# Small products of three token mixers on TensorE: other shapes and another order of the parts of the array

## The chip, the core and the metric

The kernel runs on one core of one Trainium2 chip. The metric is the device time of one execution in microseconds (us), as the median of several runs. TensorE (PE) multiplies a stationary operand, which a weight load (PEld) brings into the 128 x 128 array, with a moving operand that streams through it; results land in PSUM. VectorE (DVE), ScalarE (ACT) and GpSimd (POOL) do the elementwise work, SyncE (SP) issues the DMAs.

## What is computed

One decoder layer on 1024 tokens of width 1024, all in float32. The middle of it is three groups of heads of size 64 side by side: two chunked gated linear attentions (HGRN2 with 4 heads, GLA with 6) and RWKV-7 (6 heads).

```python
h = x * (1.0 + scale1) + shift1
z = h @ w_in[l]                                   # 1024 x 1024 by 1024 x 3984
o_h = hgrn2_mixer(z_h, ...); o_g = gla_mixer(z_g, ...); o_r = rwkv7_mixer(z_r, ...)
o = jnp.concatenate([o_h, o_g, o_r], axis=-1) @ w_out[l]
x = layer_norm(DEEPNORM_ALPHA * x + (1.0 + gate1) * o, ...)
h = x * (1.0 + scale2) + shift2
m = jnp.square(jax.nn.relu(h @ mlp_w_up[l])) @ mlp_w_down[l]     # width 4096
x = layer_norm(DEEPNORM_ALPHA * x + (1.0 + gate2) * m, ...)

# linear attention, per head and chunk
scores = jnp.einsum('bthk,bshk,btshk->bths', qc, kc, decay)      # causal
o = einsum('bths,bshv->bthv', scores, vc) + einsum('bthk,bhkv->bthv', qc * jnp.exp(b), S)
S = S * jnp.exp(b_end)[..., None] + einsum('bshk,bshv->bhkv', kc * jnp.exp(b_end[:, None] - b), vc)
# RWKV-7, per head and token
S = S * w_t + (S a_t) b_t^T + v_t k_t^T;   y_t = S r_t
```

## The kernel before

The 1024 tokens are two blocks of 512, and a block is four tiles of 128 tokens. Two kinds of work share the engines.

**Dense products** are the projections and the MLP. Each operand is split into two float32r parts, and a product is three matmuls (`mm3`, L1270 to L1272) of a 128 x 128 stationary operand and 512 moving columns, into PSUM tiles `dn` (and `tn` at the end). ACT makes the high part of a weight slab (L1220), DVE the low part (L1221).

**Mixers** run on one tile of 128 tokens at a time, in plain float32. Their matmuls are small. A float32 matmul of the program shows as two records in the trace, a transpose as one. Heads go in pairs, head a = 0 on partitions 0 to 63 and a = 1 on 64 to 127. Linear attention uses PSUM tiles `ml`, RWKV-7 `mr`, two buffers each.

- `la_blocks` (L512): scores of the second 64 tokens against the first 64. Per head one matmul of 64 rows and 64 columns, the two heads of a pair into two PSUM tiles; ACT copies them out (L515). The right factor `R` holds both heads of a pair, with zeros where a head meets the other head's rows.
- `la_attn`: the outputs of ten heads. For each pair one product of the decayed queries with the state (L475, whole array, 128 moving columns) and for each of its two heads two products of the scores `sc` with the values `V` (L482): one for the first 64 tokens on 64 rows, one for the second on 128 rows. ACT copies the sums out (L484).
- `rw_prep`: `BK` holds b~ and k~ of a chunk and a second copy of k~ (made by ACT, L585), so that both heads can take them in the order they need. The chunk products (L598) take 64 rows, 128 columns and 128 moving columns, the heads of a pair in turn.
- `rw_prep2`: `BK` transposed, head by head (L662, 64 rows), three at a time into a PSUM tile, each copied out by ACT (L664).
- `rw_chain`: after the second chunk of a tile the outputs `y`. For each head a and chunk d three products with the state (L795, a quarter of the array), then three with u and v (L798, 128 rows and half of the columns). ACT copies them out (L800).

`mixers` runs RWKV-7 a tile ahead of linear attention. `Order` sets the order of each engine's queue ahead of the run: it goes through a planned time with its own costs (`cost`), and of the instructions that are ready there it takes the one of the lowest level and the earliest traced one. The first block's mixers have level 0, and the second block's projection fills the room between them; the second block's mixers lie between chunks of the first block's MLP. Semaphores wait for data as usual.

## Time and profile before

| what | value |
|---|---|
| median of 3 runs | 1686.83 us |
| the runs | 1665.26, 1686.83, 1694.75 us |
| profiled execution, first to last instruction | 1676.5 us |
| PE busy | 1565.6 us (93%) |
| DVE, ACT, POOL busy | 65%, 41%, 25% |
| chain that ended last, by engine | PE 49%, DVE 6%, ACT 1%, POOL 1%, DMA 1% |

The profiled execution was timed by its span alone; the span lies 10.3 us below the median and inside the range of the runs. The chain that ended last could be followed back to 671.6 us. The first block's mixers lie between some 100 us and 671 us, the second block's between 671 us and 1050 us; after that there are dense products alone.

### The profile page before, as it was taken

The page shows a single profiled execution, that of the slowest core. Times are in us where ns is not written, and L with a number is a line of the kernel's source. Part 1 is how long each engine was busy: PE and PEld are TensorE (multiplying, and loading weights), DVE is VectorE, ACT ScalarE, POOL GpSimd, SP SyncE. Part 2 cuts the span into 40 slices and gives each one's busy share as a digit, 9 for nine tenths or more (in the row PEclk, how much of TensorE's full clock was granted, in tenths as well). Part 3 has the DMA queues.
Part 4 walks back from the last instruction along what each step waited for, and adds up shares of the span by engine and source line. Part 5 has one row for each costly group of instructions (what it writes and reads, how often), then busy time and mean ns, then how long its engine had stood idle before and what let it go on. Part 6 is the DMA issues. An engine that isn't in the chain of part 4 may idle for free.

```text
span 1676.5 us, 29172 instructions
## 1 busy us (share of the span) xinstructions
PE 1565.6 (93%) x11002; PEld 1220.9 (73%) x11002; DVE 1097.7 (65%) x1877; ACT 683.0 (41%) x1415; POOL 419.1 (25%) x561
## 2 busy tenths in 40 slices
PE   6998988999989998889999999999999999999996
PEld 5887766666667876657667676778888888888885
DVE  8796586666657448875857766555766954444477
ACT  3452343444344655544534543442333333333241
POOL 5224054263434132451452624100000000000003
PEclk9999996787879999898959989999999999999998
DMA  9997542313322456522313131444523643333331
GB/s 310 324 335 232 181 134 68 108 51 110 87 65 86 130 176 194 178 63 77 88 37 105 39 101 44 146 132 130 191 95 94 201 144 96 96 97 96 94 120 50
DMA packets 164892, 214.03 MB, mean 128 GB/s; under 512 B 41456, under 2 KB 91792, under 8 KB 164752
## 3 DMA queue, kind: packets, MB, share of 16 engines
q1 hardware_dynamic: 164752, 212.18, 40.5%
q8 instruction: 86, 1.41, 0.3%
q14 instruction: 54, 0.44, 0.1%
HBM read 180.07 MB, written 32.06 MB: 127 GB/s over the span
## 4 chain that ended last, share of the span: by engine, by line
PE 49%; DVE 6%; DMA 1%; issue 1%; ACT 1%; POOL 1%; SPq 0%; DVEq 0%; ACTq 0%; POOLq 0%
PE dn L1272 10%; PE dn L1271 9%; PE dn L1270 9%; PE tn L1272 4%; PE tn L1271 4%; PE tn L1270 4%; PE ml L482 1%; DVE Rs L425 1%; PE ml L475 1%; PE mr L798 1%; PE mr L795 1%; DVE xt L1401 1%; DVE wl L1221 0%; DMA lnr<-in_ln_b_dram 0%; PE ml L434 0%
## 5 line engine op out<-in xcount | busy, mean ns | idle before, releaser
L1220 ACT CAST wh<-raw 128x512 fp32r<-128x512 f32 (+2 forms) x424 | 253.2, 599 | 558.4 <-PE dn L1272 230.7
L1221 DVE TENSOR_TENSOR wl<-raw,wh 128x512 fp32r<-128x512 f32 (+2 forms) x408 | 284.8, 703 | 274.0 <-ACT wh L1220 246.0
L1270 PE MATMUL dn<-wh,ah 128*128 128x512 f32 (+1 forms) x736 | 288.0, 393 | 6.8 <-DVE xt L1417 3.8
L1271 PE MATMUL dn<-wl,ah 128*128 128x512 f32 (+1 forms) x736 | 288.0, 391 | 2.0 <-DVE wl L1221 2.0
L1272 PE MATMUL dn<-wh,al 128*128 128x512 f32 (+1 forms) x736 | 285.1, 394 | 1.8 <-DVE al L1443 1.8
L1270 PE MATMUL dn<-ah,wh 128*128 128x512 f32 x560 | 236.7, 424 | 19.6 <-ACT ah L1263 11.7
L1271 PE MATMUL dn<-al,wh 128*128 128x512 f32 x560 | 236.7, 423 | 3.2 <-DVE al L1221 1.6
L1272 PE MATMUL dn<-ah,wl 128*128 128x512 f32 x560 | 236.8, 424 | 0.0
L1270 PEld LDWEIGHTS dn<-wh,ah 128*128 128x128 f32 x736 | 140.7, 191 | 36.8 <-ACT wh L1220 3.5
L1271 PEld LDWEIGHTS dn<-wl,ah 128*128 128x128 f32 x736 | 140.3, 191 | 29.6 <-DVE wl L1221 3.4
L1272 PEld LDWEIGHTS dn<-wh,al 128*128 128x128 f32 x736 | 140.0, 191 | 29.5 <-DVE al L1443 3.2
L1270 PEld LDWEIGHTS dn<-ah,wh 128*128 128x128 f32 x560 | 111.8, 200 | 44.4 <-ACT ah L1263 11.7
L1271 PEld LDWEIGHTS dn<-al,wh 128*128 128x128 f32 x560 | 112.0, 200 | 30.3 <-DVE al L1264 4.1
L1272 PEld LDWEIGHTS dn<-ah,wl 128*128 128x128 f32 x560 | 111.8, 200 | 23.6 <-issue 0.4
L416 POOL TENSOR_TENSOR ld<-b 128x640 f32<-128x640 f32 x56 | 76.5, 1373 | 138.0 <-PE ml L512 15.3
L1458 DVE TENSOR_TENSOR xt<-xt,dn 128x512 f32<-128x512 f32 x104 | 67.1, 683 | 52.9 <-PE dn L1272 52.8
L1272 PE MATMUL tn<-ah,wl 128*128 128x512 f32 x256 | 100.8, 394 | 0.0
L1271 PE MATMUL tn<-al,wh 128*128 128x512 f32 x256 | 100.2, 391 | 0.0
L1270 PE MATMUL tn<-ah,wh 128*128 128x512 f32 x256 | 99.6, 389 | 0.0
L1518 POOL TENSOR_SCALAR lnm<-lnm 128x1 f32<-128x1 f32 x3 | 2.1, 684 | 328.5 <-DVE lnm L1516 328.5
L425 DVE TENSOR_TENSOR Rs<-ld,Q 64x320 f32<-64x320 f32 x112 | 82.0, 732 | 2.0 <-ACT ld L157 0.6
L1186 DVE SCALAR_TENSOR_TENSOR xt<-xt,xt 128x1024 f32<-128x1024 f32 x48 | 64.2, 1344 | 16.3 <-DMA xt<-in_ada_wt_dram 16.0
(290 smaller groups left out, 2500.9 us busy)
## 6 DMA issues: line engine op xcount, KB each, us to landing
raw<-in_mlp_w_up_dram SPq DMA_DIRECT2D x128, 256.0 KB
raw<-in_mlp_w_down_dram SPq DMA_DIRECT2D x128, 256.0 KB
xt<-in_ada_wt_dram SPq DMA_DIRECT2D x48, 512.0 KB
raw<-in_w_in_dram SPq DMA_DIRECT2D x64, 256.0 KB
raw<-in_w_in_dram SPq DMA_DIRECT2D x48, 192.0 KB
raw<-in_w_out_dram SPq DMA_DIRECT2D x32, 256.0 KB
raw<-in_w_in_dram SPq DMA_DIRECT2D x32, 196.0 KB
raw<-in_xt_dram SPq DMA_DIRECT2D x24, 256.0 KB
```

The lines of the kernel that those rows point to most:

```text
L416: nc.gpsimd.tensor_tensor(ev, bv, bv[:, :, h - 1:h].broadcast_to([P, 5 * nb, 2 * h]), ALU.subtract)
L425: nc.vector.tensor_tensor(Rv[half[a], a], ev[half[a], :, up], qv[half[a], :, up], ALU.mult)
L475: nc.tensor.matmul(po[:, c0:c0 + 128], qe[:, p, :], St[:, p, :], start=True, stop=False, skip_group_check=True)
L482: nc.tensor.matmul(po[half[t], c0 + 64 * a:c0 + 64 * a + 64], sc[r, 2 * p + a, half[t]], V[r, v0:v0 + 64], start=False, stop=True, skip_gr ...
L795: nc.tensor.matmul(py[half[d], p * 64:p * 64 + 64], AR[rr, p, d, 1, :], s["SU"][d][rr, p, a, :], start=(p == 0), stop=False, skip_group_ch ...
L1186: nc.vector.scalar_tensor_tensor(w, w, 1.0, self.cact, ALU.mult, ALU.mult, accum_out=self.sums[:, q:q + 1])
L1220: nc.scalar.copy(hi[:, 0:n], src)
L1221: (eng or nc.vector).tensor_tensor(lo[:, 0:n], src, hi[:, 0:n].bitcast(F32), ALU.subtract)
L1270: nc.tensor.matmul(ps, lh, rh, start=first, stop=False)
L1271: nc.tensor.matmul(ps, lh, rl, start=False, stop=False)
L1272: nc.tensor.matmul(ps, ll, rh, start=False, stop=last)
L1458: nc.vector.tensor_tensor(acc[t][:, cs], acc[t][:, cs], ps, ALU.add)
```

## The change

The same sums are computed. Six places use other shapes or another order.

```diff
 (la_attn: scores times values)
                 for a in range(2):
                     v0 = p * 128 + 64 * a
-                    for t in range(2):
-                        r = slice(0, 64 + 64 * t)
-                        nc.tensor.matmul(po[half[t], c0 + 64 * a:c0 + 64 * a + 64], sc[r, 2 * p + a, half[t]],
-                                         V[r, v0:v0 + 64], start=False, stop=True, skip_group_check=True)
+                    nc.tensor.matmul(po[:, c0 + 64 * a:c0 + 64 * a + 64], sc[:, 2 * p + a, :], V[:, v0:v0 + 64],
+                                     start=False, stop=True, skip_group_check=True)
 (la_blocks, h == 64)
-            pss = [self.lps() for _ in range(2)]
-            for p in range(5):
-                for a in range(2):
-                    r = slice(64 * a, 64 * a + 64)
-                    nc.tensor.matmul(pss[a][0:64, p * 64:p * 64 + 64], e[r, p * 128:p * 128 + 64], R[r, a, p, :],
-                                     start=True, stop=True)
-            for a in range(2):
-                nc.scalar.copy(sc[0:64, a::2, 64:128], pss[a][0:64, 0:320].rearrange("p (q t) -> p q t", q=5))
+            ps = self.lps()
+            for p, j in ((0, 0), (3, 1), (1, 0), (4, 1), (2, 0)):
+                c0 = (p - 3 * j) * 128
+                for m in range(2):
+                    s0 = 64 * j + 32 * m
+                    nc.tensor.matmul(ps[s0:s0 + 32, c0:c0 + 128], e[:, p * 128 + 32 * m:p * 128 + 32 * m + 32],
+                                     R[:, :, p, :], start=True, stop=True)
+            for j, h0, h1 in ((0, 0, 6), (1, 6, 10)):
+                nc.scalar.copy(sc[0:64, h0:h1, 64:128], ps[64 * j:64 * j + 64, 0:64 * (h1 - h0)]
+                               .rearrange("p (q t) -> p q t", t=64))
 (rw_prep)
-        BK = self.mt([P, 3, 2, 3, 64], "BK")
+        BK = self.mt([P, 3, 2, 2, 64], "BK")
...
-        nc.scalar.copy(BKm[:, :, 2, :], BKm[:, :, 0, :])
...
             for p in range(3):
-                for a in range(2):
-                    rr = slice(64 * a, 64 * a + 64)
-                    nc.tensor.matmul(pxs[a][:, p * 128:(p + 1) * 128],
-                                     BK[rr, p, c, 1 - a:3 - a, :].rearrange("p x t -> p (x t)"),
-                                     AR[rr, p, c].rearrange("p x t -> p (x t)"), start=True, stop=True)
+                for x in range(2):
+                    for a in range(2):
+                        rr = slice(64 * a, 64 * a + 64)
+                        r = slice(64, 128) if a ^ x else slice(0, 64)
+                        nc.tensor.matmul(pxs[a][r, p * 128:(p + 1) * 128], BK[rr, p, c, x, :],
+                                         AR[rr, p, c].rearrange("p x t -> p (x t)"), start=True, stop=True)
 (rw_prep2, per chunk c)
-            for a in range(2):
-                rr = slice(64 * a, 64 * a + 64)
-                pt = self.mps()
-                for p in range(3):
-                    nc.tensor.transpose(pt[:, p * 64:(p + 1) * 64],
-                                        BK[rr, p, c, 1 - a:3 - a, :].rearrange("p x t -> p (x t)"), self.ident[rr, rr])
-                nc.scalar.copy(BT[:, a], pt[:, 0:192].rearrange("p (q d) -> p q d", d=64))
+            pt = self.mps()
+            for p in range(3):
+                nc.tensor.transpose(pt[:, p * 128:(p + 1) * 128], BK[:, p, c].rearrange("p x t -> p (x t)"), self.ident)
+            pt3 = pt[:, 0:384].rearrange("p (q d) -> p q d", d=128)
+            nc.scalar.copy(BT[:, 0], pt3[:, :, 0:64])
+            for x in range(2):
+                nc.scalar.copy(BT[64 - 64 * x:128 - 64 * x, 1], pt3[64 * x:64 * x + 64, :, 64:128])
 (rw_chain, c == 1)
+            pys = [self.mps() for _ in range(2)]
+            for p in range(3):
+                for d, a in ((0, 0), (1, 1), (0, 1), (1, 0)):
+                    rr = half[a]
+                    nc.tensor.matmul(pys[a][half[d], p * 64:p * 64 + 64], AR[rr, p, d, 1, :], s["SU"][d][rr, p, a, :],
+                                     start=(p == 0), stop=False, skip_group_check=True)
             for a in range(2):
-                rr = half[a]
-                py = self.mps()
-                for d in range(2):
-                    for p in range(3):
-                        nc.tensor.matmul(py[half[d], p * 64:p * 64 + 64], AR[rr, p, d, 1, :], s["SU"][d][rr, p, a, :],
-                                         start=(p == 0), stop=False, skip_group_check=True)
-                    for p in range(3):
-                        nc.tensor.matmul(py[half[d], p * 64:p * 64 + 64], s["E"][d][:, a, p, 64:128],
+                for p in range(3):
+                    for d in range(2):
+                        nc.tensor.matmul(pys[a][half[d], p * 64:p * 64 + 64], s["E"][d][:, a, p, 64:128],
                                          s["UV"][d][:, p, a, :], start=False, stop=True, skip_group_check=True)
```

In the changed kernel the lines are numbered a little differently: L482 becomes L480, L598 L600, L662 L661, L798 L800, and the dense products L1272 to L1274; L475, L512 and L795 keep their numbers. Per tile of tokens the program has 10 products of scores and values instead of 20, 10 score products of the far block as before, 24 chunk products instead of 12, 6 transposes of `BK` instead of 12, and 24 output products as before. ACT loses the copy of k~ and has 6 copies out of the transposes instead of 4.

The order is planned anew by the same rules. PE at the outputs of linear attention, the second block's third tile, before (names are PSUM tile, moving and stationary operand; the size is that of the output):

```order
L475 MATMUL ml_9446<-st,ld_9434 128x128
L482 MATMUL ml_9446<-V_8774,sc 64x64 x4
L475 MATMUL ml_9446<-st,ld_9434 128x128
L482 MATMUL ml_9446<-V_8774,sc 64x64 x4
L475 MATMUL ml_9446<-st,ld_9434 128x128
L482 MATMUL ml_9446<-V_8774,sc 64x64 x4
L475 MATMUL ml_9463<-st,ld_9434 128x128
L482 MATMUL ml_9463<-V_8774,sc 64x64 x4
```

and of the changed kernel at the same place, where the whole transposes L661 now lie between:

```order
L480 MATMUL ml_9419<-V_8743,sc 128x64 x2
L475 MATMUL ml_9419<-st,ld_9407 128x128
L480 MATMUL ml_9419<-V_8743,sc 128x64 x2
L475 MATMUL ml_9419<-st,ld_9407 128x128
L480 MATMUL ml_9419<-V_8743,sc 128x64 x2
L661 MATMUL mr_9178<-consts,BK_8816 128x128 x3
L480 MATMUL ml_9430<-V_8743,sc 128x64 x2
L661 MATMUL mr_9186<-consts,BK_8816 128x128 x3
L475 MATMUL ml_9430<-st,ld_9407 128x128
L480 MATMUL ml_9430<-V_8743,sc 128x64 x2
```

Four products per pair of heads became two, and all of this stretch has one form, that of the dense products beside it. PE at the RWKV-7 outputs, the second block's second tile, before (`SU` is the state, `UV` u and v):

```order
L795 MATMUL mr_8327<-SU_7133,AR_7274 64x64 x3
L798 MATMUL mr_8327<-UV_7613,E_7290 64x64 x3
L795 MATMUL mr_8327<-SU_7618,AR_7274 64x64 x3
L798 MATMUL mr_8327<-UV_7619,E_7301 64x64 x3
L795 MATMUL mr_8341<-SU_7133,AR_7274 64x64 x2
L1270 MATMUL dn_10594<-wh_10597,ah_10565 128x512
```

and of the changed kernel there:

```order
L795 MATMUL mr_8313<-SU_7120,AR_7255 64x64
L795 MATMUL mr_8313<-SU_7610,AR_7255 64x64
L795 MATMUL mr_8313<-SU_7120,AR_7255 64x64
L795 MATMUL mr_8313<-SU_7610,AR_7255 64x64
L795 MATMUL mr_8313<-SU_7120,AR_7255 64x64
L795 MATMUL mr_8313<-SU_7610,AR_7255 64x64
L800 MATMUL mr_8313<-UV_7605,E_7270 64x64
L800 MATMUL mr_8313<-UV_7611,E_7287 64x64
L800 MATMUL mr_8313<-UV_7605,E_7270 64x64
L800 MATMUL mr_8313<-UV_7611,E_7287 64x64
```

The two chunks, which write the two halves of the partitions, now take turns, and six products of one form stand together; the planner still finishes one PSUM tile before the other.

## Rows read from the trace of the kernel before

**Rows 1.** The page: span, and busy time of two engines.

```profile
span 1676.5 us, 29172 instructions
PE 1565.6 (93%) x11002; PEld 1220.9 (73%) x11002; DVE 1097.7 (65%) x1877; ACT 683.0 (41%) x1415; POOL 419.1 (25%) x561
```

**Rows 2.** Windows of three stretches: length, busy time of PE, PEld, DVE, ACT, POOL, granted clock.

```profile
210.00:671.00 461.00, 421.67 (x3893) 315.85 (x3893) 298.66 (x550) 217.97 (x506) 177.25 (x259) 0.86 0.37 110
671.00:1050.00 379.00, 349.05 (x3555) 255.93 (x3554) 268.81 (x458) 177.36 (x412) 158.82 (x204) 0.87 0.27 81
1050.00:1634.00 584.00, 580.26 (x2568) 473.13 (x2567) 342.36 (x538) 198.44 (x331) 6.01 (x6) 1.00 0.40 124
```

**Rows 3.** Groups on PE by line and shape: stationary, moving, records, busy us, mean ns.

```profile
L482 PE MATMUL ml<-V,sc 64*64 64x64 f32 x160 | 32.5, 297 | 0.0
L482 PE MATMUL ml<-V,sc 128*64 128x64 f32 x160 | 32.3, 302 | 0.0
...
L475 PE MATMUL ml<-st,ld 128*128 128x128 f32 x80 | 25.3, 412 | 15.4 <-DVE ld L460 15.4
...
L798 PE MATMUL mr<-UV,E 128*64 128x64 f32 x192 | 22.9, 256 | 0.0
L598 PE MATMUL mr<-AR,BK 64*128 64x128 f32 x192 | 22.5, 337 | 9.9 <-ACT BK L585 9.6
L795 PE MATMUL mr<-SU,AR 64*64 64x64 f32 x192 | 22.2, 250 | 2.3 <-DVE UV L778 2.3
L662 PE MATMUL mr<-consts,BK 64*128 64x64 f32 x96 | 15.3, 296 | 0.8 <-ACT BT L664 0.6 <-DVE bon L651 0.3
L781 PE MATMUL mr<-UV,BT 128*64 128x64 f32 x192 | 14.7, 240 | 0.4 <-DVE UV L778 0.3
...
L512 PE MATMUL ml<-Rs,ld 64*64 64x64 f32 x160 | 10.5, 236 | 2.6 <-DVE Rs L425 2.4
...
L775 PE MATMUL mr<-sm,TW 64*64 64x64 f32 x192 | 9.4, 232 | 0.3
```

**Rows 4.** Timeline of PE, outputs of one pair of heads and the next pair's start.

```profile
966.15 0.49 PE L475 MATMUL ml<-st,ld 128*128 128x128 f32 x2
966.56 1.10 PE L482 MATMUL ml<-V,sc 64*64 64x64 f32 x8
967.59 0.49 PE L475 MATMUL ml<-st,ld 128*128 128x128 f32 x2
```

**Rows 5.** Timeline of PE, the same in another tile.

```profile
758.00 0.80 PE L475 MATMUL ml<-st,ld 128*128 128x128 f32 x2
758.73 2.70 PE L482 MATMUL ml<-V,sc 64*64 64x64 f32 x14
```

**Rows 6.** Windows as in the second group, around four places of the timeline.

```profile
758.00:760.00 2.00, 2.00 (x10) 1.43 (x10) 0.00 (x0) 0.00 (x0) 0.00 (x0) 0.50 0.00 0
966.00:968.00 2.00, 2.00 (x14) 1.43 (x14) 1.99 (x3) 0.53 (x2) 2.00 (x2) 1.00 0.48 106
980.80:981.60 0.80, 0.80 (x22) 0.73 (x21) 0.70 (x2) 0.12 (x1) 0.00 (x0) 1.00 0.00 0
1260.00:1262.00 2.00, 2.00 (x19) 1.87 (x18) 2.00 (x4) 0.63 (x1) 0.00 (x0) 1.00 0.41 131
```

**Rows 7.** Timeline of PE: state products (L497), and whole transposes ahead of the MLP.

```profile
980.80 0.80 PE L497 MATMUL ml<-V,ld 128*64 128x64 f32 x20
...
1260.29 1.91 PE L1235 MATMUL tn<-consts,xt 128*128 128x128 f32 x16
1261.95 0.48 PE L1270 MATMUL dn<-ah,wh 128*128 128x512 f32 x1
```

**Rows 8.** ACT's copy of k~, as a group.

```profile
L585 ACT COPY BK<-BK 128x384 f32<-128x384 f32 x8 | 4.1, 512 | 10.6 <-DVE BK L584 10.6
```

**Rows 9.** Waits of PE: us in total, times, longest.

```profile
PE ml L475 <- DVE ld L460: 15.4, 6, 5.9
...
PE mr L598 <- ACT BK L585: 9.6, 4, 3.1
```

More of the change, by code (lines that the diff above doesn't have):

```diff
@@ L577, in rw_prep @@
         nc.gpsimd.tensor_tensor(b, kk, aa, ALU.mult)
-        nc.vector.tensor_tensor(BKm[:, :, 1, :], c6(b), c6(eb), ALU.mult)
+        nc.vector.tensor_tensor(BKm[:, :, 0, :], c6(b), c6(eb), ALU.mult)
         k2 = wk()
@@ L583, in rw_prep @@
         nc.vector.tensor_tensor(k2, k2, k, ALU.mult)
-        nc.vector.tensor_tensor(BKm[:, :, 0, :], c6(k2), c6(eb), ALU.mult)
-        nc.scalar.copy(BKm[:, :, 2, :], BKm[:, :, 0, :])
+        nc.vector.tensor_tensor(BKm[:, :, 1, :], c6(k2), c6(eb), ALU.mult)
         el = self.mt([P, 3, 2, 1], "el", 2)
@@ L789, in rw_chain @@
             y = self.mt([P, 6, 64], "wp", 2)
-            for a in range(2):
-                rr = half[a]
-                py = self.mps()
-                for d in range(2):
-                    for p in range(3):
-                        nc.tensor.matmul(py[half[d], p * 64:p * 64 + 64], AR[rr, p, d, 1, :], s["SU"][d][rr, p, a, :],
-                                         start=(p == 0), stop=False, skip_group_check=True)
-                    for p in range(3):
-                        nc.tensor.matmul(py[half[d], p * 64:p * 64 + 64], s["E"][d][:, a, p, 64:128],
+            pys = [self.mps() for _ in range(2)]
[4 more added lines that the diff above has]
+                                     start=(p == 0), stop=False, skip_group_check=True)
+            for a in range(2):
+                for p in range(3):
+                    for d in range(2):
+                        nc.tensor.matmul(pys[a][half[d], p * 64:p * 64 + 64], s["E"][d][:, a, p, 64:128],
                                          s["UV"][d][:, p, a, :], start=False, stop=True, skip_group_check=True)
-                nc.scalar.copy(y[:, a::2, :], py[:, 0:192].rearrange("p (q d) -> p q d", d=64))
+                nc.scalar.copy(y[:, a::2, :], pys[a][:, 0:192].rearrange("p (q d) -> p q d", d=64))
             s["y"] = y
```

## The prediction

> **What bounds the kernel now.** I read the page first: PE is busy for 1565.6 of 1676.5 us, VectorE for 65%, ScalarE for 41% [rows 1]. Then windows over three stretches [rows 2]. From 1050 us on PE is busy for 580.26 of 584 us at full clock with dense products that the change does not touch. In the two stretches with the mixers it is busy for 421.67 of 461 us and 349.05 of 379 us, which leaves 39 + 30 = 69 us idle, and the granted clock is 0.86 and 0.87. Since the clock has two levels, 1.2 and 2.4 GHz, that is 0.28 x 461 + 0.26 x 379 = 228 us at half clock. So time must come out of PE's queue in these 840 us, by less work, or by the same work at the higher clock.
>
> The groups by shape [rows 3] show which small products are dear. One shape, 128*64 with 64 moving columns, costs 32.3 / 160 = 0.20 us a record at L482 and 14.7 / 192 = 0.077 us at L781. The timeline tells why: twenty records of this shape in a row take 0.80 us, 0.04 each [rows 7], while eight records of L482 stretch from 966.56 to 967.59, 0.129 each [rows 4], both at full clock [rows 6]. L482 goes from a 64*64 to a 128*64 form and back with every product; L497 keeps its form and only changes halves. The array pays for each change of form, nearly 0.1 us, and after it nothing overlaps. L475 between them is dear for the same reason: two records hold PE from 966.15 to 966.56, 0.205 each, where sixteen whole-array transposes with as many moving columns take 1.66 us, 0.104 each [rows 4, 7].
>
> **The change part by part.** All 8 tiles together, PE time.
>
> *Outputs of linear attention (L475 and L482).* 5 pairs by 8 tiles are 40 pairs of heads. At full clock a pair takes 967.59 - 966.15 = 1.44 us [rows 4]. At half clock L475 takes 0.73 and fourteen records of L482 2.70 us, so eight take 1.54: 2.27 us a pair [rows 5, 6]. With half of the pairs at either clock that is 40 x 1.86 = 74 us; the groups' own sum, 32.5 + 32.3 + 25.3 = 90 us [rows 3], counts ends twice. Afterwards a pair has 2 records of L475 and 4 of L480, all whole-array and in the form of the dense products beside them. No row has a whole-array float32 record with 64 moving columns. Below, half of the transposes' 0.104, if only the columns count: 2 x 0.104 + 4 x 0.052 = 0.42 us. Above, L475's 0.205 for each of six: 1.23 us. I take 0.104 for all six, the price of one whole-array record whose form doesn't change, with its load of 128 columns: 0.62 us at full and 1.25 at half clock, 37 us in all. Saved: 37 us; between the ends 5 (1.23 and 2.2) and 49 (0.42 and 0.83).
>
> Here the Trainium skill speaks against the change. Its page "TensorE: Matmul & The Clock Gate", section "Part 3: Packing small matmuls — row/col tiling", says that a weight load overlaps a running matmul only where the row groups differ. The whole-array products use all rows, so by it each would pay its load and its columns one after the other, and the part would save some 5 us rather than 37. The trace disagrees as far as it goes: L497's records use all 128 rows too, and twenty of them with twenty loads take 0.80 us [rows 7].
>
> *RWKV-7 outputs (L795, L798).* 22.2 + 22.9 = 45.1 us for 384 records, 0.117 each [rows 3]. Now they run in the same quarter or half three at a time and change form between threes; afterwards the two halves take turns, six products and more of a form together. The nearest rows of the same two shapes, where parts take turns, are L775, 9.4 / 192 = 0.049, and L781, 0.077 [rows 3]: 9.4 + 14.7 = 24 us. Saved 21. Best, 384 x 0.04 [rows 7] = 15: saved 30. Worst, L795 as it is and L798 as L781: saved 8.
>
> The outputs now hold both `mr` buffers until ScalarE has copied them out. If the next RWKV-7 products, and the dense ones queued behind them, wait for that, it is two copies a tile of at most 0.512 us [rows 8], 8 us in all; I take 0, since the order still finishes one PSUM tile before the other.
>
> *Transposes of BK (L662).* 96 records, 15.3 us [rows 3], most in threes of a 64-row form between dense products. 48 whole ones at 0.104 to 0.208 (half clock), mean 0.156, are 7.5 us. Saved 8; 10 if all run at full clock, 2 at L475's 0.205 and twice that at half clock.
>
> *Chunk products (L598).* 192 records, 22.5 us [rows 3], two row halves at a time. The 384 new ones are quarters with the same 128 moving columns. If four quarters run together, 22.5 us again; if they go two together, 0.098 each by twice L775's price: 37.6, a loss of 15; one after the other 45, a loss of 22. Best is 4 gained (four at once at L775's price for 64 columns). The order takes the two diagonal quarters, then the other two, so I lean to four: a loss of 4.
>
> *Far scores (L512).* As many records, 10.5 us [rows 3], with twice the moving columns but four column groups in place of two row halves. I take 0; a loss of 10 if the columns decide, a gain of 5 if twice as many run at once.
>
> *ScalarE.* The copy of k~ goes, 8 x 0.512 us [rows 8]; PE waited for it four times, 9.6 us in all [rows 9], of which VectorE's write before it stays. I take 4 x 0.5 = 2 us gained, 0 to 5. The transposes have two more copies a tile; ScalarE, 41% busy, hides them [rows 1], and if it doesn't, eight tiles with 2 x 0.3 us are 5 us.
>
> The sum is 37 + 21 + 8 - 4 + 0 + 2 = 64 us of PE time; the ends are -25, with the buffers' wait, and 103.
>
> *What is late next.* PE's idle time has DVE behind it: L475 waits 15.4 us for the decayed queries [rows 9], and no DVE instruction is dropped. A PE that gets there sooner waits longer. I give back a quarter, 16 us. On the other side dense products in half-clock stretches gain when such a stretch gets shorter: a product takes half as long at full clock. In each of eight tiles the outputs' stretch shrinks from 5 x 1.86 = 9.3 to 4.7 us; if half of what is cut was at half clock and the chip leaves that clock as much earlier, dense work gains some 1 us a tile, 8 us in all. Net: 64 - 16 + 8 = 56 us. From the profiled span of 1676.5 us, which was timed by itself alone, that gives 1620; the median of the runs lies 10 above the span, so I predict **1631 us**, 0.967 of the median. The three runs span 1.8%, so 2% is about what a measurement of this kernel can tell from no change.
>
> **The rivals.**
>
> *The chain of the mixers decides (no change).* In the first block the mixers come first in the plan, and the projection only fills. If there the wait for DVE and POOL takes all that PE saves, only the second block's half pays: 32 us, less a quarter, 24. That gives 1676.5 - 24 + 10 = 1663. For it: 39 us idle in this stretch, and the waits on DVE. Against it: PE is busy for 91% there, at a mean clock of 0.86 [rows 2].
>
> *Whole-array records don't hide their loads (no change).* By the skill's rule above. In rows: six records at L475's price save 5 instead of 37. The sum falls to 32, less its quarter 24, and without the 8: 1663 again.
>
> *The change doesn't do what it says: parts run one after the other.* Each unknown at its bad end, -25 us: 1676.5 + 25 + 10 = 1712.
>
> *Slower by the clock.* PE saves its 64 us, waits for DVE instead, and a PE with gaps is granted the half clock for longer; the dense products between then run at half speed. Each us more at half clock loses 0.5 us of full-clock work. It eats the net gain of 56 when half clock grows by 112 us, from 228 to 340 of the 840 us; at 450 the time is 1676.5 - 56 + 111 + 10 = 1742. For it: the clock is low in the mixers' stretches and full beside them, where PE is never idle [rows 2]. Against it: at 758 us PE is busy without a gap and has half clock all the same [rows 6], so sparse products are part of what goes with it, and these are what shrinks.
>
> *The clock recovers (faster still).* By the same row: if half of the 228 us goes, 114 us of half clock give 57 us back instead of my 8, and less idle is lost: 64 - 16 + 57 = 105, so 1676.5 - 105 + 10 = 1582.
>
> **How the numbers follow.** Forecast, 1608 to 1653: 0.57. The chain decides: 0.17. Loads not hidden: 0.08. Parts in a row: 0.04. Slower by the clock: 0.04. The clock recovers: 0.10. The range must leave out no more than 0.2: it takes the forecast and both cases at 1663 with some spread, and from the faster case the near half, 1592 to 1672. Faster by over 2% means below 1653: nearly all of the forecast, the recovered clock, and a little of the chain's case, 0.69. Within 2%: the rest of the two cases at 1663, the case of parts in a row, and the forecast's edge, 0.25. Slower: 0.06, the clock and the far end of the parts in a row.
>
> **What would show it.** In the profile of the changed kernel a pair of L475 and L480 should take 0.6 to 0.7 us at full clock where nothing comes between, against 1.44; over 1 us says that loads aren't hidden. L795 and L800 together should be busy for about 24 us, L661 for 8, L600 for 22 to 30, L512 for 10. The copy L585 is gone from PE's waits. PE's idle time in the mixers' stretches should be 69 to 85 us and their clock 0.86 or higher. If idle time grows by 50 us or more, the chain decided; if the clock falls below 0.8, the clock did. Wrong would also be a saving that is there in the first block and not in the second, where PE has the MLP to go on with and nothing but its own work sets the pace.

## The result: 0.9585 of the time before, and the profile after

The changed kernel takes 1606.62 us (median of 4 runs, 1602.05 to 1611.46), the kernel before 1680.66 us (4 runs, 1665.26 to 1694.75): a ratio of 0.9585, 95% interval 0.9534 to 0.9635. The forecast was 1631 us, 0.967, with a range of 1592 to 1672. Direction and range held; the gain is 74 us where 56 were forecast, and the time lies just below the forecast's own band of 1608 to 1653 us, towards the rival in which the clock recovers.

The page of the changed kernel, span and busy time, then windows of the mixers' two stretches with the columns of [rows 2]:

```profile
span 1600.0 us, 29147 instructions
...
PE 1483.7 (93%) x10986; PEld 1165.7 (73%) x10986; DVE 1089.5 (68%) x1877; ACT 685.4 (43%) x1423; POOL 423.8 (26%) x561
```

```profile
210.00:671.00 461.00, 414.98 (x4406) 313.74 (x4405) 335.73 (x616) 246.38 (x568) 207.53 (x297) 0.92 0.43 127
671.00:1050.00 379.00, 348.32 (x3371) 265.11 (x3370) 270.94 (x461) 183.76 (x412) 136.12 (x169) 0.93 0.31 90
```

Against [rows 1, 2] PE's busy time fell by 81.9 us and its idle time rose by 5.3 (1676.5 - 1565.6 = 110.9, 1600.0 - 1483.7 = 116.3). The windows' clock rose from 0.86 and 0.87 to 0.92 and 0.93. They are the same stretches of time, not of work: in the changed kernel the last state products of the eighth tile come at 976.8 us in place of 1051.0, so its second window ends in dense products. From 210 us to the end of its mixers, 977 us, the clock is 0.92 and PE is idle for 73 us (before, to 1051 us: 0.87 and 69 us).

The groups that answer to [rows 3], and the timeline of one pair of heads, which answers to [rows 4]:

```profile
L480 PE MATMUL ml<-V,sc 128*128 128x64 f32 x160 | 26.7, 295 | 0.0
L600 PE MATMUL mr<-AR,BK 64*64 64x128 f32 x384 | 23.6, 292 | 14.6 <-DVE BK L579 12.6 <-DVE E L603 1.4 <-DVE BK L585 0.5
L475 PE MATMUL ml<-st,ld 128*128 128x128 f32 x80 | 19.3, 335 | 17.9 <-DVE ld L460 17.8
...
L795 PE MATMUL mr<-SU,AR 64*64 64x64 f32 x192 | 11.7, 247 | 2.4 <-DVE SU L786 1.5 <-DVE UV L779 0.9
L800 PE MATMUL mr<-UV,E 128*64 128x64 f32 x192 | 11.0, 255 | 0.0
L512 PE MATMUL ml<-Rs,ld 128*32 128x128 f32 x160 | 10.2, 299 | 0.9 <-DVE Rs L425 0.9
...
L661 PE MATMUL mr<-consts,BK 128*128 128x128 f32 x48 | 9.0, 302 | 2.3 <-DVE bon L652 2.3
```

```profile
500.42 0.44 PE L475 MATMUL ml<-st,ld 128*128 128x128 f32 x2
500.70 0.56 PE L480 MATMUL ml<-V,sc 128*128 128x64 f32 x4
501.09 0.44 PE L475 MATMUL ml<-st,ld 128*128 128x128 f32 x2
```

A pair takes 501.09 - 500.42 = 0.67 us in place of 1.44 [rows 4], 0.111 a record on average, and 0.62 had been taken. The reader should not add up the groups' busy times here: the mean of an L480 record is 295 ns, while six records fit into 670 ns. So the next table counts each record of PE from its start to the next record's start, or to its own end where a gap follows. These sums make up PE's busy time exactly.

| PE time, us | before | of it at half clock | after | of it at half clock | saved | forecast |
|---|---|---|---|---|---|---|
| outputs of linear attention (L475, L482; L475, L480) | 76.3 | 52.0 | 31.4 | 11.7 | 45 | 37 |
| RWKV-7 outputs (L795, L798; L795, L800) | 39.4 | 13.8 | 20.3 | 6.9 | 19 | 21 |
| transposes (L662; L661) | 13.2 | 9.9 | 5.9 | 1.8 | 7 | 8 |
| chunk products (L598; L600) | 21.3 | 9.9 | 21.6 | 3.0 | 0 | -4 |
| far scores (L512) | 9.7 | 2.5 | 8.8 | 1.7 | 1 | 0 |
| dense products and all other records | 1405.7 | 137.1 | 1395.7 | 108.6 | 10 | 8 |
| idle | 110.9 | | 116.3 | | -5 | -14 |
| span | 1676.5 | | 1600.0 | | 77 | 56 |

The forecast's -14 is the quarter given back (-16) and the copy's 2. Busy time at half clock fell from 225 to 134 us, and the same work needs half of that at full clock: 46 of the 82 us of busy time are clock, 36 are work. Worked out in the same way for each row, 32 of the 72 us that the five parts saved are clock. The chunk products' nothing is 4 us more of work against 3 us of clock, and the 10 us of the other records are 14 of clock against 4 more of work.

**Where the half clock went.** Windows of 25 us from the start of the outputs of each of the eight tiles, PE alone (length, busy time, granted clock, DMA share and GB/s); of the kernel before, then of the changed one:

```profile
275.00:300.00 25.00, 24.09 (x102) 0.53 0.27 84
379.00:404.00 25.00, 24.08 (x119) 0.60 0.21 51
474.00:499.00 25.00, 23.83 (x113) 0.59 0.24 65
549.00:574.00 25.00, 25.00 (x166) 0.99 0.31 90
752.00:777.00 25.00, 24.38 (x119) 0.73 0.20 61
865.00:890.00 25.00, 24.53 (x124) 0.73 0.24 62
964.00:989.00 25.00, 24.27 (x130) 0.80 0.34 93
1039.00:1064.00 25.00, 24.16 (x140) 0.96 0.10 28
```

```profile
279.00:304.00 25.00, 24.53 (x144) 0.93 0.52 169
358.00:383.00 25.00, 23.86 (x139) 0.93 0.42 130
440.00:465.00 25.00, 24.76 (x307) 0.86 0.47 146
499.00:524.00 25.00, 24.89 (x164) 1.00 0.46 140
692.00:717.00 25.00, 24.20 (x121) 0.80 0.27 80
807.00:832.00 25.00, 24.15 (x145) 1.00 0.39 118
894.00:919.00 25.00, 24.56 (x182) 0.93 0.46 133
968.00:993.00 25.00, 24.40 (x141) 1.00 0.36 105
```

A window's half-clock time is 2 x (1 - clock) x 25 us. The eight sum to 104 us before and 28 after: 76 of the 87 us by which half clock fell in the whole span (mean clock 0.928 of 1676.5 us is 241 us, 0.952 of 1600.0 is 154).

The two blocks gain unequally. Up to the last state products of the fourth tile (560.6 us before, 506.6 after) the changed kernel is 54 us ahead, and from there to those of the eighth tile it gains 20 us more. Half clock falls from 137 to 61 us in the first stretch and from 96 to 79 in the second. In the profiled run of e1 below the two gains are 49 and 14 us.

The second of these tiles shows an example. Timeline of PE, before and after (start, length, records, idle time ahead in brackets):

```profile
375.02 0.39 PE L1271 MATMUL dn<-al,wh 128*128 128x512 f32 x1
379.92 0.77 PE L475 MATMUL ml<-st,ld 128*128 128x128 f32 x2 [4.51 <-DVE ld L460]
380.61 1.68 PE L482 MATMUL ml<-V,sc 64*64 64x64 f32 x8
...
391.80 0.87 PE L482 MATMUL ml<-V,sc 64*64 64x64 f32 x4
392.60 0.80 PE L1272 MATMUL dn<-ah,wl 128*128 128x512 f32 x1
```

```profile
354.27 0.40 PE L1272 MATMUL dn<-ah,wh 128*128 128x512 f32 x1
358.42 0.46 PE L475 MATMUL ml<-st,ld 128*128 128x128 f32 x2 [3.75 <-DVE ld L460]
358.63 0.48 PE L1273 MATMUL dn<-al,wh 128*128 128x512 f32 x1
```

Windows around them, columns as above, before and after:

```profile
379.00:399.00 20.00, 19.08 (x85) 0.50 0.17 43
399.30:402.00 2.70, 2.70 (x24) 1.00 0.23 56
```

```profile
359.20:362.40 3.20, 3.20 (x12) 0.50 0.52 122
362.60:366.00 3.40, 3.40 (x26) 1.00 0.59 190
```

In both kernels PE waits for VectorE's decayed queries, 4.51 and 3.75 us, and the granted clock falls around its end (by the clock records at 378.8 us, in the wait, and at 359.1, just behind it). In the kernel before a train of outputs follows that takes from 379.92 to 392.60 us, and the clock is low until 399.2. In the changed one dense and whole-array products follow, in the order that was planned anew, and the clock is back at 362.5. The wait is much the same; what follows it is not. Ahead of the eight tiles' outputs as a whole PE waits no less than before, 17.8 us against 15.4 [rows 9].

### The profile page after: what moved, and what is told of

It is laid out like the page before. It is cut to its first block, busy times and chain, and to the rows that moved or that the text cites. A ratio compares the mean times of both kernels' runs of the same rounds, so it can differ in the third digit from the quotient of the medians.

```text
span 1600.0 us, 29147 instructions
## 1 busy us (share of the span) xinstructions
PE 1483.7 (93%) x10986; PEld 1165.7 (73%) x10986; DVE 1089.5 (68%) x1877; ACT 685.4 (43%) x1423; POOL 423.8 (26%) x561
## 4 chain that ended last, share of the span: by engine, by line
PE 48%; DVE 7%; ACT 2%; DMA 2%; issue 1%; POOL 1%; SPq 0%; DVEq 0%; ACTq 0%; POOLq 0%
PE dn L1274 10%; PE dn L1272 10%; PE dn L1273 9%; PE tn L1273 5%; PE tn L1272 5%; PE tn L1274 5%; DVE wl L1223 1%; DVE Rs L425 1%; DMA lnr<-in_ln_b_dram 1%; DVE xt L1403 1%; DVE ld L420 0%; DVE al L1445 0%; DMA raw<-oD 0%; DVE zm L269 0%; PE mr L800 0%
## 5 line engine op out<-in xcount | busy, mean ns | idle before, releaser
L1223 DVE TENSOR_TENSOR wl<-raw,wh 128x512 fp32r<-128x512 f32 (+2 forms) x408 | 294.1, 725 | 260.6 <-ACT wh L1222 238.2
L1272 PE MATMUL dn<-wh,ah 128*128 128x512 f32 (+1 forms) x736 | 286.7, 392 | 6.1 <-DVE xt L1419 2.8
L1274 PE MATMUL dn<-wh,al 128*128 128x512 f32 (+1 forms) x736 | 284.0, 392 | 2.0 <-DVE al L1445 2.0
L1272 PE MATMUL dn<-ah,wh 128*128 128x512 f32 x560 | 236.1, 423 | 17.9 <-ACT ah L1265 12.0
L1274 PE MATMUL dn<-ah,wl 128*128 128x512 f32 x560 | 235.5, 422 | 0.7 <-DVE wl L1223 0.7
L1272 PEld LDWEIGHTS dn<-wh,ah 128*128 128x128 f32 x736 | 140.2, 191 | 36.3 <-DVE xt L1419 3.7
L1274 PEld LDWEIGHTS dn<-wh,al 128*128 128x128 f32 x736 | 139.8, 191 | 29.4 <-DVE al L1445 3.5
L1272 PEld LDWEIGHTS dn<-ah,wh 128*128 128x128 f32 x560 | 111.3, 199 | 44.1 <-ACT ah L1265 12.0
L1274 PEld LDWEIGHTS dn<-ah,wl 128*128 128x128 f32 x560 | 110.7, 198 | 25.5 <-issue 1.8
L1272 PE MATMUL tn<-ah,wh 128*128 128x512 f32 x256 | 101.0, 394 | 0.0
L1274 PE MATMUL tn<-ah,wl 128*128 128x512 f32 x256 | 100.4, 392 | 0.0
L425 DVE TENSOR_TENSOR Rs<-ld,Q 64x320 f32<-64x320 f32 x112 | 70.8, 632 | 1.3
```

The costliest lines, as they stand in the source:

```text
L425: nc.vector.tensor_tensor(Rv[half[a], a], ev[half[a], :, up], qv[half[a], :, up], ALU.mult)
L1223: (eng or nc.vector).tensor_tensor(lo[:, 0:n], src, hi[:, 0:n].bitcast(F32), ALU.subtract)
L1272: nc.tensor.matmul(ps, lh, rh, start=first, stop=False)
L1274: nc.tensor.matmul(ps, ll, rh, start=False, stop=last)
```

## Experiments

Twelve kernels are told by what they tell apart; half-clock time is 2 x (1 - mean clock) x span. The runs of one kernel lie 13 to 73 us apart in it, and the profiled run is one of them, sometimes the lowest (e7) or the highest (e3). So comparisons go by the last column, the median of the runs with the lowest and the highest, and less than some 20 us of difference says nothing. Each experiment has its edit and what had been expected of it.

| kernel | median us | ratio to before, 95% | profiled span | its mean clock | its half clock, us | half clock of the runs, us |
|---|---|---|---|---|---|---|
| before | 1680.66 | 1 | 1676.5 | 0.928 | 241 | 248 (216 to 284, 44 runs) |
| changed kernel | 1606.62 | 0.9585 (0.9534 to 0.9635) | 1600.0 | 0.952 | 154 | 159 (147 to 164) |
| e1: scores times values alone | 1612.28 | 0.9575 (0.9507 to 0.9644) | 1612.1 | 0.950 | 161 | 156 (134 to 174) |
| e2: RWKV-7 outputs alone | 1670.12 | 0.9947 (0.9903 to 0.9991) | 1668.2 | 0.923 | 257 | 254 (218 to 291) |
| e4: the other parts alone | 1666.49 | 0.9929 (0.9890 to 0.9968) | 1679.4 | 0.928 | 242 | 211 (189 to 255) |
| e11: e1 and e2 together | 1605.33 | 0.9575 (0.9530 to 0.9621) | 1598.4 | 0.946 | 173 | 171 (167 to 180) |
| e3: before, grouped by form | 1631.03 | 0.9700 (0.9636 to 0.9764) | 1636.8 | 0.931 | 226 | 202 (168 to 226) |
| e8: the same, sums kept | 1628.81 | 0.9672 (0.9611 to 0.9734) | 1629.6 | 0.939 | 199 | 189 (168 to 199) |
| e5: changed, whole-array dose | 1638.01 | 0.9736 (0.9676 to 0.9797) | 1631.9 | 0.952 | 157 | 170 (157 to 181) |
| e7: changed, dose of quarters | 1644.72 | 0.9760 (0.9688 to 0.9832) | 1628.7 | 0.962 | 124 | 174 (124 to 178) |
| e9: changed, dose of form changes | 1625.15 | 0.9699 (0.9629 to 0.9769) | 1621.4 | 0.955 | 146 | 148 (139 to 156) |
| e10: before, whole-array dose | 1681.26 | 1.0024 (0.9978 to 1.0069) | 1690.0 | 0.936 | 216 | 197 (181 to 230) |
| e6: changed, halves in turn | 1608.69 | 0.9571 (0.9498 to 0.9644) | 1601.4 | 0.955 | 144 | 158 (141 to 174) |
| e12: changed, scores first | 1603.95 | 0.9567 (0.9529 to 0.9605) | 1600.8 | 0.957 | 138 | 138 (115 to 148) |

### Which part pays: e1, e2, e4, e11

e1 is the kernel before with this edit alone:

```diff
-                    for t in range(2):
-                        r = slice(0, 64 + 64 * t)
-                        nc.tensor.matmul(po[half[t], ...], sc[r, 2 * p + a, half[t]], V[r, v0:v0 + 64], ...)
+                    nc.tensor.matmul(po[:, ...], sc[:, 2 * p + a, :], V[:, v0:v0 + 64], ...)
```

> Only the scores times values are changed (one whole-array product per head, L480 of the changed kernel); the rest is as before. If the change of form inside each product was what cost, L475 and its products fall from 90 us busy to about 46, as in the changed kernel, and the span falls by 38 to 50 us, a ratio of 0.97 to 0.978, with the half-clock time down from 245 us by 50 or more. If the mixers' chain of DVE and POOL set the pace in the first block, the busy time falls as much and the span by 20 to 25 us only (0.985 to 0.99), with PE's idle time up by 20.

e2 is the kernel before with the RWKV-7 outputs in turns (shown are the products with the state; those with u and v take turns as in the change):

```diff
-                for d in range(2):
-                    for p in range(3):
-                        nc.tensor.matmul(py[half[d], ...], AR[rr, p, d, 1, :], s["SU"][d][rr, p, a, :], ...)
+            for p in range(3):
+                for d, a in ((0, 0), (1, 1), (0, 1), (1, 0)):
+                    nc.tensor.matmul(pys[a][half[d], ...], AR[half[a], p, d, 1, :], s["SU"][d][half[a], p, a, :], ...)
```

> Only the order of the RWKV-7 outputs is changed: six products of one form together, the halves in turn. Same products, same shapes. If forms and turns count, L795 and L798 fall from 45 to 23 us busy and the span by 15 to 25 us (0.985 to 0.991). If the number and shape of products counts, nothing moves (0.997 to 1.003). If holding both PSUM buffers of RWKV-7 costs a wait, the busy time falls and the span doesn't.

e4 has the other parts, with the shapes of BK that they need (the loops are shortened here):

```diff
-                    nc.tensor.matmul(pxs[a][:, ...], BK[rr, p, c, 1 - a:3 - a, :], ...)
+                    for x in range(2): nc.tensor.matmul(pxs[a][r, ...], BK[rr, p, c, x, :], ...)
-                    nc.tensor.transpose(pt[:, p * 64:(p + 1) * 64], BK[rr, p, c, 1 - a:3 - a, :], self.ident[rr, rr])
+                nc.tensor.transpose(pt[:, p * 128:(p + 1) * 128], BK[:, p, c], self.ident)
-                    nc.tensor.matmul(pss[a][0:64, ...], e[r, ...], R[r, a, p, :], ...)
+                    for m in range(2): nc.tensor.matmul(ps[s0:s0 + 32, ...], e[:, ...], R[:, :, p, :], ...)
```

> The changed kernel with scores times values and the RWKV-7 outputs put back to the kernel before; left are the quarters of the chunk products, the whole transposes, the copy of k~ that is gone, and the far scores in column groups. By the sum of busy times (transposes 6 us less, chunk products 1 more, far scores the same, PE's wait for the copy a few us shorter) the span falls by 5 to 12 us (0.993 to 0.997). If these parts set off the clock as well, by 20 us or more (0.988 or less). If the extra copies of ScalarE on the way to the chain count, it rises by up to 5 us.

e11 holds the edits of e1 and e2:

> The kernel before with two parts of the change alone, whole-array scores times values and the outputs of RWKV-7 in turns; transposes, chunk products and far scores as before. If the parts add up: 1681 - 68 - 10 = 1603. If the clock is regained once and what PE saves more is lost to waits: as the first part alone, 1607 to 1615. Either way the difference from the whole change, 1607, says what the other three parts are worth beside these two: between -4 and +8 us.

Measured: scores times values alone bring 68 us, nearly the whole gain and more than the 38 to 50 expected, and take half clock from 248 to 156 us. The RWKV-7 outputs alone shorten their records from 39.4 to 22.2 us, 17 us, and the kernel by 10, less than the 15 to 25 expected; half clock stays. The other parts alone bring 14 us by the median, a little more than expected, and half clock falls to 211 us. The parts' sum, 68 + 10 + 14 = 92 us, is more than the whole's 74, by a little more than the intervals allow. Whether the second part adds to the first, e11 doesn't tell: 1605.33 us lies between the 1603 and the 1607 expected. e11 has the whole's time without the other parts. In the profiled runs they take 7.5 us of PE time off it (1491.2 to 1483.7), and idle time grows by 9 (107.2 to 116.3), so there the saving turned into waiting. Between e1, e11 and the changed kernel the intervals overlap, and no order among them is claimed.

### Form changes or whole-array products: e3 and e8

The kernel before with its products of quarters and halves, ordered by form within each PSUM group:

```diff
             for p in range(p0, p1):
                 nc.tensor.matmul(po[:, c0:c0 + 128], qe[:, p, :], St[:, p, :], start=True, ...)
-                for a in range(2):
-                    for t in range(2):
-                        nc.tensor.matmul(po[half[t], ...], sc[r, 2 * p + a, half[t]], V[r, v0:v0 + 64], ...)
+            for t in range(2):
+                for q in range(2 * p0, 2 * p1):
+                    nc.tensor.matmul(po[half[t], ...], sc[r, q, half[t]], V[r, q * 64:q * 64 + 64], ...)
```

In e3 the later state products start the sums anew, so the state part of a group's earlier pairs is missing from its output; instructions and shapes are the same. e8 starts only the first (`start=(p == p0)`) and loses nothing.

> The kernel before with the same 20 products of scores and values per tile, of the same two shapes, but in groups: first the state products of three (or two) pairs, then all products of the first 64 tokens, then all of the second 64. The forms change three times a group and not four times a pair. If the change of form is the cost, a record of L482 falls from 0.13 us at full clock to 0.06, the three pairs take some 0.8 us each where they took 1.44, and the span falls by 20 to 35 us (0.98 to 0.988). If the number of products or the 64 moving columns are the cost, nothing moves (0.997 to 1.003) and only halving the products, as the change does, helps.

> The grouped triangle again, the kernel before with its twenty products of scores and values a tile ordered by form, all state products of a group first, then the quarters, then the halves, here with the sum of the state products kept. Same instructions as the earlier grouped kernel but for one flag: 0.965 to 0.975 of the kernel before, about 1630, half-clock time 210 to 235 us.

Both agree: 49 and 52 us faster, more than the 20 to 35 first expected, though no product of scores and values is whole. Records of one form now mostly follow each other in 0.058 us at full clock; before, 0.107 us lay between the two records of a product and 0.148 to 0.152 at a change of form. The mean of all of them at full clock is 0.076 us in place of 0.125, and the outputs need 49.4 us of PE time (e8) in place of 76.3. So the changes of form were a large part of the cost, as the prediction read from [rows 4, 7]. Half clock falls too, to 202 and 189 us, some two thirds of the way from 248 to e1's 156 (e8), and 17 to 19 us are missing to e1. In windows of the profiled run of e8 like those above four tiles are at low clock, and the other four at 0.95 to 1.00:

```profile
273.00:298.00 25.00, 24.72 (x132) 0.66 0.30 96
368.00:393.00 25.00, 24.54 (x134) 0.66 0.25 65
463.00:488.00 25.00, 24.12 (x142) 0.73 0.34 94
...
826.00:851.00 25.00, 24.75 (x129) 0.66 0.28 73
```

The eight sum to 67 us, against 104 and 28. Grouping leaves few form changes, but in these four tiles, where PE waits 2.1 to 4.3 us ahead of the outputs, the half clock lasts 13.7 to 17.1 us, 7 to 8 of them outputs. In the other four it waits 0.9 us or less.

### What the clock hangs on: e5, e7, e9, e10

Four kernels add about the same PE time, 25 to 31 us by starts of records. e5 issues each state product of the changed kernel four times:

```diff
+                for _ in range(4):
                     nc.tensor.matmul(po[:, c0:c0 + 128], qe[:, p, :], St[:, p, :], start=True, ...)
```

> The changed kernel with every whole-array state product (L475) issued four times in a row, each restarting the sum, so the result stays as it is. That is 15 more records of two loads and two passes a tile, 30 x 0.111 us x 8 tiles = 27 us of PE at full clock; the form never changes and PE has no new wait. Theory that PE's own time sets the end: 27 to 35 us slower than the changed kernel's 1607, that is 1634 to 1642, ratio 0.972 to 0.977, with half-clock time as it was (150 us or less). Rival, the chain of the mixers decides and PE has room beside it: at most 15 us slower, 1622 or less.

e7 and e9 put other products ahead of the state products, which overwrite them:

```diff
+            for _ in range(17 if n == 3 else 11):                        (e7)
+                nc.tensor.matmul(po[half[0], 0:64], sc[half[0], 2 * p0, half[0]], V[half[0], ...], ...)
+            for x in range(8 if n == 3 else 6):                          (e9)
+                r = slice(0, 64 + 64 * (x % 2))
+                nc.tensor.matmul(po[half[x % 2], 0:64], sc[r, 2 * p0, half[x % 2]], V[r, ...], ...)
```

> The changed kernel with 28 more products a tile on one quarter of the array (64 rows, 64 columns, 64 moving columns) ahead of the state products, which overwrite them. All are in the same quarter, so none overlaps another: by the start-to-start times of such records, 0.058 us each at full clock, 56 records x 0.058 x 8 tiles = 26 us, with about 3 us for the changes of form: nearly the same PE time as the kernel with repeated whole-array products. If PE time alone counts, both are equally slow, 1634 to 1642. If the granted clock follows how much of the array works, this one is slower by 10 us or more than the other, and has at least 20 us more half-clock time.

> The changed kernel with 14 extra products a tile ahead of the state products, which overwrite them: a quarter (64 rows by 64 columns) and a half (128 rows by 64 columns) in turn, so that the form changes with each product, as it did in the kernel before. By that kernel's start-to-start times, 0.12 us a record at full clock, 28 records x 0.12 x 8 tiles = 27 us: the same PE time as the doses of repeated state products and of quarters, which cost 31 and 38 us and left half-clock time at 156 and 125 us. If PE time alone counts: 1632 to 1647 and half-clock time of 125 to 165 us. If trains of products that change form are what went with the half clock: half-clock time of 180 us or more, and 1650 to 1670.

e10 has e5's edit in the kernel before.

> The kernel before with every state product of the linear attention issued four times in a row, each restarting the sum: 15 more whole-array products a tile in the midst of the trains that change form. 30 records x 0.111 us x 8 tiles = 27 us at full clock, 51 us if all of them run at the half clock that the trains have there. If the trains' half clock comes with their form changes and whole-array products beside them don't lift it: 1710 to 1735. If whole-array products in the trains bring the full clock back, half-clock time falls from 243 us to 200 or less, and the kernel is at most 15 us slower than before, 1695 or less.

e5 costs 31 us for 25 us of PE time: here what PE works is paid in full, and the rival that it has room is out. e7 costs 38 us by the medians (profiled runs: 29) for 31 us of PE time, 7 us more than e5, and its half clock is e5's, 174 us against 170; the 124 us of the profiled run are the lowest of its four. So no lowering of the clock by products on a quarter of the array shows in such trains of 2 us. e9 costs 19 us for 28 us of PE time, less than the 25 or more expected, and its half clock, 148 us, is that of the changed kernel: form changes in trains of 2 to 3 us don't lower it either. Both have a flaw that I had not seen ahead: their extra products stand where PE waits for the decayed queries (L475's idle time of 17.9 us shrinks to 9.1 and 6.0 us), so they also remove idle time, after which the clock had fallen.

e10 is the surprise: 28 us more PE time in the kernel before, and its time does not change (1.0024, 0.9978 to 1.0069). The half clock of its ten runs has a median of 197 us against 248, and 51 us less of half clock are worth 25 us, about what was added. The profiled run has 216 us, more than most of the ten, and in its eight windows 65 us against 104:

```profile
273.00:298.00 25.00, 23.94 (x149) 0.80 0.25 75
364.00:389.00 25.00, 24.97 (x110) 0.55 0.26 68
...
976.00:1001.00 25.00, 24.95 (x165) 1.00 0.36 99
```

By the profiled runs the dose costs 13.5 us of its 28, by the medians nothing. So less half clock goes with whole-array products in the trains, though the trains get longer (12.2 to 22.9 us against 8.3 to 13.2); not in every tile, as the second window shows. Both bounds set for this case, 200 us of half clock and 1695 us, were met by the medians.

### Is there more to gain: e6 and e12

e6 cuts each whole-array product of the changed kernel into its column halves, in turn, after the group's state products:

```diff
-                    nc.tensor.matmul(po[:, ...], sc[:, 2 * p + a, :], V[:, v0:v0 + 64], ...)
+            for q in range(2 * p0, 2 * p1):
+                for t in range(2):
+                    nc.tensor.matmul(po[half[t], ...], sc[:, q, half[t]], V[:, q * 64:q * 64 + 64], ...)
```

> The changed kernel with each whole-array product of scores and values cut into its two column halves (128 rows by 64 columns), issued in turn after the state products of the group, so that one change of form is paid a group instead of one a product. Twice as many records; if two halves work at once as they do in the twenty products of L497, 0.04 us a record, a pair of heads takes 2 x 0.111 + 8 x 0.04 = 0.54 us at full clock against 0.67. Theory that whole and half products cost what their records last: 3 to 6 us faster than the changed kernel, or equal, 1600 to 1608. Rival, what made the grouped triangle of products slow (its low clock) comes from products on part of the array: then this is slower than the changed kernel, 1612 to 1630, with more than 175 us of half-clock time.

```profile
502.13 0.71 PE L475 MATMUL ml<-st,ld 128*128 128x128 f32 x4
502.77 1.38 PE L480 MATMUL ml<-V,sc 128*64 128x64 f32 x38
504.08 0.45 PE L1273 MATMUL dn<-wl,ah 128*128 128x392 f32 x1
```

38 records take 1.31 us, 0.034 each, where a whole-array record takes 0.111. PE is busy for 14 us less than in the changed kernel (1469.4), and the time is the same: idle time rose from 116 to 132 us. The half clock of the runs is 158 us as in the changed kernel (159), and the profiled run's eight windows lie at 0.90 to 1.00: products on half of the array, the halves in turn, keep the clock as whole ones do. The rival is out.

e12 has the scores' products ahead of the state products (L475 is now scores times values, L479 the state products):

```diff
+            for q in range(2 * p0, 2 * p1):
+                nc.tensor.matmul(po[:, ...], sc[:, q, :], V[:, q * 64:q * 64 + 64], start=(q == 2 * p0), ...)
             for p in range(p0, p1):
                 nc.tensor.matmul(po[:, c0:c0 + 128], qe[:, p, :], St[:, p, :], start=False, ...)
```

> The changed kernel with the two kinds of products of a group in the other order: all scores times values first, then the state products, which wait for VectorE's decayed queries (L475 waited 17.9 us for them in all). Same products, same forms. In the kernels with extra quarters or forms ahead of the state products that wait was 9.1 and 6.0 us, so work placed there lies beside it. If PE's waits for VectorE decide what is left: some 9 us faster than the changed kernel, 1595 to 1602, ratio 0.949 to 0.954. Rival, the wait only moves to the next product that takes VectorE's results: 1603 to 1611, as the changed kernel.

```profile
PE ml L434 <- DVE Rs L425: 18.8, 15, 2.5
...
PE mr L599 <- DVE BK L578: 11.3, 6, 2.8
PE ml L479 <- DVE ld L460: 10.0, 3, 4.8
PE mr L660 <- DVE bon L651: 7.7, 4, 3.0
```

The wait for the queries is 10.0 us in place of 17.8, but the transposes (L660) wait 7.7 us in place of 2.3, L434 18.8 in place of 16.5, and idle time is 122 us. The time, 1603.95 us, lies within the interval of the changed kernel: the wait has moved, as the rival had it.

## Why the prediction was right, and where its sizes were off

- **What bounds the kernel.** PE's queue in the mixers' stretches: right. 25 us of PE time cost e5 31 us, and the gain came from there: of 76.5 us of span 74 lie ahead of the last state products. The price isn't always full: e9's 28 us cost 19 beside a wait, and e10's 28 us nothing as the clock rose.
- **Outputs of linear attention.** The mechanism is shown: a form change per product cost (e8), whole-array records follow in 0.111 us on average, a pair takes 0.67 us. Sized at 37 us, it brought 45. The working priced half of the pairs at half clock before and after, which is 61% and 67% of their time. Before that was a little low: 52.0 of 76.3 us ran at half clock; after it was far too much, 11.7 of 31.4.
- **The rule on loads.** By the price that the prediction gave its rival, six records at L475's 0.205 us, a pair would have taken some 1.23 us. The trace shows 0.67. At full clock nearly all weight loads of these outputs start 0.11 us after the one before, whether their record moves 64 or 128 columns, so a load doesn't wait for the columns of the record ahead of it. The sentence that the prediction took from the Trainium skill ("TensorE: Matmul & The Clock Gate", "Part 3: Packing small matmuls — row/col tiling") was not borne out for records that all use the whole array. The same section also lets a load go ahead where it targets the background weight buffer. The loads' 0.11 us fit that, but no run shows the buffer.
- **RWKV-7 outputs, transposes, chunk products, far scores.** 19, 7, 0 and 1 us against 21, 8, -4 and 0: within the bounds. Where four quarters of the chunk products come in a row they do run together: from 113.99 us on four records start within 0.02 us, and the next four 0.11 us after the first of them. Without the clock's part the chunk products lost 4 us, as taken. Alone the RWKV-7 outputs brought 10 us of time (e2); e11 and the whole don't tell their worth beside the first part from nothing.
- **The copy of k~.** It is gone from PE's waits, but 2 us gained was wrong: L600 waits 14.6 us for what L598 waited 9.9, of it 12.6 for VectorE's own write (L579).
- **What is late next.** The quarter given back was too much: -14 with the copy's 2, measured -5. Idle time did not grow in proportion to what PE saved; the further savings of e6 and e12, and that of the other parts beside e11, were lost to it.
- **The clock: the step that failed.** "Dense work gains some 1 us a tile, 8 us in all" is the size for the other records, 10 us, but the clock was worth 46 us of busy time, some two thirds of it inside the parts. The rival "the clock recovers" had the mechanism: it let 114 of 228 us of half clock go, and 87 of 241 went (89 of 248 by the medians of the runs). I gave it 0.10: from [rows 6] I read that sparse products are a part of what goes with half clock, and did not look at what stands ahead of the long low stretches with outputs in them, mostly a wait and then a train. Its own sum, 105 us, counted the clock twice, since the parts' 64 us already held some of it.
- **What adds up.** The difference of 20 us between 77 and 56 is 10 for the parts (8 of them the first), 9 for idle time and 2 for the clock of the rest, by the rows of the table, each rounded.
- **The two blocks.** The rivals halved the saving between the blocks. The first had 54 us of it and the second 20, and the half clock went with it (75 and 17 us less). That leans to what the prediction named as a sign of being wrong, a saving in the first block and none in the second; the second did gain, but less than it took.
- **The low end.** It leaves out the 5 us of ScalarE's copies, and its transposes save 0.5 us rather than 2 at the prices given: some -31 us in place of -25. The rival of parts in a row would move by that from 1712 to some 1718; the forecast doesn't.
- **The other signs and rivals.** The pair's 0.67 us, L795 and L800 with 22.7 us busy, L661 with 9.0, L600 with 23.6, L512 with 10.2, the idle time of 73 us and the clock of 0.92 in the mixers' stretch are as the prediction said. The chain decides: not for this change, as the first block gained most, but what e6 and e12 save goes into waits. Loads not hidden, parts in a row, slower by the clock: none came.

What stays open is why the half clock went: whether the trains kept it by their length, by their form changes or by how little of the array they use. With e8's order by form, which also shortens the trains, some two thirds of it went, so form changes alone are not all; e6 says not by half-array products in turn; e10 that whole-array products among them help. No kernel puts a long train of quarters behind a wait without also filling that wait. Nor was the order held: each kernel is planned anew, and in the changed one 22.7 of 54.1 us from the first to the last output of the tiles are other records, against 12.8 of 89.0 before, so part of the gain can be the plan's.

## What to carry to other kernels

Before costing small products by their busy time, look at the granted clock around them and at what stands ahead of each fall: a wait and then a long train of small, form-changing products can pay twice: 46 of the 82 us of busy time that the change saved here were clock. Price records by their distance from start to start, and price the clock before and after apart, since the share of half clock is a result of the change and not a given. Once the trains are short, further savings of TensorE can turn into waits, as in e6 and e12, so the engine that TensorE waits for is the next to look at.

## What had not been expected of the hardware

- 28 us of added whole-array products left the time as it was (e10, 1.0024, 0.9978 to 1.0069), while half clock fell by 51 us (248 to 197, medians of the runs).
- Whole-array float32 records follow each other in 0.111 us on average, with 64 moving columns as with 128, as their weight loads start that far apart; two column halves in turn take 0.034 us each (38 records in 1.31 us), less for the pair than the one whole record.
- A wait of 4.5 us was followed by 20.4 us of half clock before (378.8 to 399.2), a wait of 3.75 us by 3.4 us after the change (359.1 to 362.5); what PE had to do next differed, a train of outputs before, dense and whole-array products after.
